# A transformer layer on one core: parameter rows and lambdas behind the first norm's root, and the conditioning's sums over partitions by transposes

## Chip, core and metric

One core of a Trainium2 chip. The metric is the device time of one execution in microseconds; three runs of the kernel before gave 1547.67 us in the median (1547.43 to 1552.2).

## What is computed

One layer over 256 tokens of width 2048 in float32, with adaptive norms: a vector c gives, through a large matrix w_mod, a shift, a scale and a gate for each of the two halves of the layer.

```python
cond = silu(c)
mod = cond @ w_mod[l] + b_mod[l]                       # (1, 6 * 2048)
sh1, sc1, gt1, sh2, sc2, gt2 = split(mod, 6)
u = modulate(rms_norm(h, norm1_g[l]), sh1, sc1)        # norm * (1 + scale) + shift
aq, ak, av, rq, rf, ri, rg, ga, gr = split_columns(u @ w_in[l])
lam = exp(sum(lambda_q1 * lambda_k1)) - exp(sum(lambda_q2 * lambda_k2)) + lam_init
ya = diff_attention(aq, ak, av, lam, subln_g[l], lam_init)
yr = hgrn2(rq, rf, ri, rg, lower_bounds[l], gnorm_g[l])
merged = sigmoid(ga) * (ya @ w_att_out[l]) + sigmoid(gr) * (yr @ w_rec_out[l])
h = h + gt1 * (merged @ w_o[l])
u = modulate(rms_norm(h, norm2_g[l]), sh2, sc2)
h = h + gt2 * ((silu(u @ w_ffn_gate[l]) * (u @ w_ffn_up[l])) @ w_ffn_down[l])
return rms_norm(h, final_g)
```

## The kernel before

Every large product is done three times in float32r: a weight tile w is split into a high part wh (a cast on ScalarE, L240) and a low part wl (a subtraction on VectorE, L242), the left side into uH and uL, and `products` (L245) issues for each k tile of 128 and each of the two token tiles the matmuls uH x wh, uH x wl and uL x wh. Split tiles lie in four buffers each, weights in three, accumulators in four banks (two groups of 512 columns).

**The first norm and its conditioning.** `rstd1` (L348) sums the squares of x on ScalarE, eight activations with accumulation of 128x512, and takes the root in a chain of small VectorE instructions (`rstd_of`, L196). `norm1` (L358) scales x by the root (xn), transposes it on TensorE and copies it to xT. The shift and scale come from `mod_cols` (L391), a generator. It streams its part of w_mod, multiplies each row of 128 by its entry of cond and adds up over k on VectorE into two tiles modc, one for the shift and one for the scale (L403, L407). Each modc holds 128 partial sums per column, one per partition, and these are summed over the partitions by `col_sum` (L333): for each block of 128 columns an fp32 matmul with modc as the weights and a column of ones, which leaves the sums as a column in the bank pmc. Then L426 to L428 add bias, 1 and the norm's gain, and `modulated` (L378) makes u, uH and uL from xT.

**Chunks.** The first seven projections are done in four chunks over k (`kchunks`: 3, 4, 5 and 4 tiles of 128), so that the first can start when a part of the conditioning is there. In a chunk, `chunk_cols` (L467) runs 14 groups of 512 columns with 18, 24, 30 or 24 matmuls each, and while it does, the conditioning of the next chunk runs beside it. That is an order written out by hand: `group` calls `step` (L266) behind the products of each piece of weights; `step` adds `pace["cond"]` to an account and resumes the generator once for each whole unit in it (`advance`, L258). The pace is AHEAD (1.15) times the number of loads over the number of steps (L475). A resumption of `mod_cols` goes as far as the next yield: one load, or one load and the sums for two. Behind the last chunk step `drain` resumes what is left. The conditioning of the second norm (`mod_cols(0, KA, 3, ...)`, L721, and the two of KREST, L842) runs in the same way beside later products, the rows of the gates in `mod_rows`.

The first norm's conditioning of chunk 0 is resumed by hand: two resumptions, then x is loaded, the parameter rows, and the root is taken; then 14 more, of which all but two put their VectorE instructions behind the root's last (`issue_after(last_rstd[0])`, L703). `load_rows` (L139) brings 57 rows of parameters and 96 of b_mod, transposes both on TensorE and copies them to cols and bcols on ScalarE. `lambdas` (L177) loads four vectors and takes two sums and an Exp, then `small_params` (L162) takes a softmax of two rows with another Exp; that generator is appended to the side work.

A planner orders the instructions of each engine: it takes them by the order in which the program traces them, as far as their inputs and buffers are there by its own reckoning, so that one may be moved ahead of another that is still waiting. `issue_after(ins)` puts what the block traces on the engine of `ins` behind it. Each engine works through its queue in order.

Of the kernel before, what the change touches and what calls it, by code (L numbers as in the profile page):

```python
# [8 lines left out]
F32 = mybir.dt.float32  # L9
# [3 lines left out]
AF = mybir.ActivationFunctionType  # L13
# [5 lines left out]
P = 128  # L19
D = 2048  # L20
S = 256
KT = D // P
# [29 lines left out]
def block_kernel(  # L52
# [7 lines left out]
    nc = tc.nc  # L60
# [13 lines left out]
    def bigt(name, dt=F32, n=1):  # L74
        r = [big.tile([P, 1024], dt, tag="big", name=f"{name}{i}") for i in range(n)]
        return r[0] if n == 1 else r

    def bank(name):
        return ps.tile([P, 512], F32, tag="ps", name=name)
# [42 lines left out]
    def quarter(tiles, g):  # L122

        return tiles[g // 2][:, (g % 2) * NG:(g % 2 + 1) * NG]
# [14 lines left out]
    def load_rows():  # L139
        rows = tmp.tile([P, P], F32, tag="side", name="rows", bufs=NS)  # L140
        brows = tmp.tile([P, P], F32, tag="side", name="brows", bufs=NS)
        nc.scalar.dma_start(out=brows[:nbrow, :], in_=b_mod.rearrange("o (k p) -> (o k) p", p=P))
        for r0, n, ap in (
            (0, 16, norm1_g.rearrange("o (k p) -> (o k) p", p=P)),
            (16, 16, norm2_g.rearrange("o (k p) -> (o k) p", p=P)),
            (32, 16, lb_logits.rearrange("o (k p) -> (o k) p", p=P)),
            (48, 8, gnorm_g.rearrange("o h p -> (o h) p")),
            (56, 1, subln_g),
        ):
            nc.scalar.dma_start(out=rows[r0:r0 + n, :], in_=ap)  # L150
        pc = bank("pc")
        nc.tensor.transpose(out=pc[:, :nrow], in_=rows[:nrow, :], identity=ident[:nrow, :nrow])
        nc.tensor.transpose(out=pc[:, P:P + nbrow], in_=brows[:nbrow, :], identity=ident[:nbrow, :nbrow])
        nc.scalar.copy(out=cols, in_=pc[:, :nrow])
        nc.scalar.copy(out=bcols, in_=pc[:, P:P + nbrow])
# [21 lines left out]
    def lambdas():  # L177

        lv = tmpt("lv", S).rearrange("p (i d) -> p i d", d=64)
        for i, ap in enumerate((lambda_q1, lambda_q2, lambda_k1, lambda_k2)):  # L180
            nc.scalar.dma_start(out=lv[:, i, :], in_=ap.to_broadcast([P, 64]))
        for _ in range(6):
            yield
        nc.vector.tensor_mul(out=lv[:, 0:2], in0=lv[:, 0:2], in1=lv[:, 2:4])
        ls = small.tile([P, 2], F32, tag="s2", name="ls")
        nc.vector.reduce_sum(out=ls, in_=lv[:, 0:2], axis=AX.X)
        nc.scalar.activation(ls, ls, AF.Exp)

        nc.vector.tensor_sub(out=lam[:, 0:1], in0=ls[:, 0:1], in1=ls[:, 1:2])
        nc.vector.tensor_scalar_add(out=lam[:, 0:1], in0=lam[:, 0:1], scalar1=LAM_INIT)  # L190
        nc.vector.tensor_scalar_mul(out=lam[:, 1:2], in0=lam[:, 0:1], scalar1=-1.0)
        small_params()
# [3 lines left out]
    def rstd_of(ssq, n, width, name, eps=None):  # L196

        def new(x):
            return small.tile([P, n], F32, tag=f"r{n}", name=name + x, bufs=6)

        v, y = new("v"), new("y")
        if eps is None:
            nc.vector.tensor_scalar(out=v, in0=ssq, scalar1=1.0 / width, scalar2=EPS, op0=ALU.mult, op1=ALU.add)
        else:
            nc.vector.scalar_tensor_tensor(out=v, in0=ssq, scalar=1.0 / width, in1=eps, op0=ALU.mult, op1=ALU.add)
        yi = y.bitcast(I32)
        nc.vector.tensor_single_scalar(out=yi, in_=v.bitcast(I32), scalar=1, op=ALU.arith_shift_right)
        nc.vector.tensor_scalar(out=yi, in0=yi, scalar1=-1.0, scalar2=float(0x5F3759DF), op0=ALU.mult, op1=ALU.add)
        vh = new("h")
        nc.vector.tensor_scalar_mul(out=vh, in0=v, scalar1=-0.5)  # L210
        for i in range(3):
            q, y2 = new(f"q{i}"), new(f"y{i}")
            if n == 1:
                nc.vector.scalar_tensor_tensor(out=q, in0=y, scalar=y, in1=vh, op0=ALU.mult, op1=ALU.mult)
            else:
                nc.vector.tensor_mul(out=q, in0=y, in1=y)
                nc.vector.tensor_mul(out=q, in0=q, in1=vh)
            last_rstd[:] = [nc.vector.scalar_tensor_tensor(out=y2, in0=q, scalar=1.5, in1=y, op0=ALU.add, op1=ALU.mult).ins]
            y = y2
        return y  # L220
# [37 lines left out]
    def advance(queue):  # L258
        while queue:
            try:  # L260
                next(queue[0])
                return
            except StopIteration:
                queue.pop(0)
# [68 lines left out]
    def col_sum(p, j0, a, n):  # L333
        for j in range(n):
            mm(p[:, j0 + j:j0 + j + 1], a[:, j * P:(j + 1) * P], ones[:, 0:1], start=True, stop=True)  # L335
# [6 lines left out]
    def square_sum(dst, src):  # L342
        return nc.scalar.activation(junk[:, :src.shape[-1]], src, AF.Square, accum_out=dst)  # L343

    xT, uH_t, uL_t = [], [], []
    xTv, uH, uL = halves(xT), halves(uH_t), halves(uL_t)

    def rstd1(xt):  # L348

        s8 = small.tile([P, 2, 4], F32, tag="s8", name="ssq")  # L350
        for t in range(2):
            for g in range(4):
                square_sum(s8[:, t, g:g + 1], quarter(xt[t], g))
        s2 = small.tile([P, 2], F32, tag="s2", name="ssq1")
        nc.vector.reduce_sum(out=s2, in_=s8, axis=AX.X)
        return rstd_of(s2, 2, D, "n1")

    def norm1(xt, rr, g):  # L358

        for t in range(2):  # L360
            xn = tmpt("xn")
            nc.scalar.activation(xn, quarter(xt[t], g), AF.Copy, scale=rr[:, t:t + 1])
            p = bank("pxT")
            for j in range(4):
                nc.tensor.transpose(out=p[:, j * P:(j + 1) * P], in_=xn[:, j * P:(j + 1) * P], identity=ident)
            nc.scalar.copy(out=xT[g].rearrange("p (k s) -> p k s", s=S)[:, :, t * P:(t + 1) * P], in_=p.rearrange("p (k s) -> p k s", s=P))
# [24 lines left out]
    def mod_cols(k0, nk, chunk, gcol, src, H, L, after=None, room=0, lag=0):  # L391

        wid = nk * P
        a = [tmp.tile([P, 1024], F32, tag="modc", name=f"modc{ci}", bufs=2) for ci in range(2)]
        waiting = []

        def sums(q, kk, ci, w):
            for j in range(kk):  # L400
                s1, d = cond[:, q + j:q + j + 1], a[ci][:, :wid]
                if q + j == 0:
                    first = nc.vector.tensor_scalar_mul(out=d, in0=w[:, j], scalar1=s1)  # L403
                    if after is not None:
                        tc.add_manual_dep(first.ins, after.ins.name, NOSYNC, reason="the norm goes first")
                else:
                    nc.vector.scalar_tensor_tensor(out=d, in0=w[:, j], scalar=s1, in1=d, op0=ALU.mult, op1=ALU.add)  # L407

        for q, kk in mod_loads(nk):
            for ci in range(2):  # L410
                waiting.append((q, kk, ci, load_mod(q, kk, (chunk + ci) * D + k0 * P, wid, q >= room)))
                if ci == 0:
                    yield
            while len(waiting) > (lag if q < room else 0):
                sums(*waiting.pop(0))
            yield
        for w in waiting:
            sums(*w)
        p = bank("pmc")
        for ci in range(2):  # L420
            col_sum(p, ci * nk, a[ci], nk)
        for _ in range(GAP if chunk else GAP1):
            yield
        ks = slice(k0, k0 + nk)
        bc = [bcols[:, (chunk + ci) * KT + k0:(chunk + ci) * KT + k0 + nk] for ci in range(2)]
        nc.vector.tensor_add(out=sh_col[:, ks], in0=p[:, 0:nk], in1=bc[0])  # L426
        nc.vector.tensor_add(out=sc_col[:, ks], in0=p[:, nk:2 * nk], in1=bc[1])
        nc.vector.scalar_tensor_tensor(out=sc_col[:, ks], in0=sc_col[:, ks], scalar=1.0, in1=gcol[:, ks], op0=ALU.add, op1=ALU.mult)  # L428
        if src is not None:
            for k in range(k0, k0 + nk):  # L430
                modulated(src(k, slice(0, S)), k, H, L)
# [264 lines left out]
    for _ in range(XAT):  # L696
        next(first)
    x1 = load_x()
    load_rows()
    with tc.issue_after(cond_act.ins):  # L700
        r1 = rstd1(x1)
    for i in range(XAT2):
        with tc.issue_after(last_rstd[0]) if i >= 2 else ExitStack():  # L703
            next(first, None)
    side.append(lambdas())
    advance(side)
    xT += bigt("xT", n=4)
    for g in range(4):
        norm1(x1, r1, g)
    uH_t += bigt("uH", F32R, 4)  # L710
    uL_t += bigt("uL", F32R, 4)
    for _ in first:
# [220 lines left out]
```

## Time and profile before

| | |
|---|---|
| median of three runs | 1547.67 us |
| the profiled execution | 1543.71 us, of which its span is 1541.5 us |
| mean granted TensorE clock | 0.998 |
| matmuls (PE) busy | 1495.4 us, 97% |
| weight loads (PEld) busy | 1233.7 us, 80% |
| VectorE (DVE) busy | 1101.4 us, 71% |
| ScalarE (ACT) busy | 732.4 us, 48% |
| DMA | 373.67 MB, 242 GB/s over the span |

The profile is of one execution, 4 us shorter than the median of the runs; what is summed up from its rows is compared with its own time. Busy shares are means over all stages. What an engine waited for, and who waited for it, stands in the views of waits, and the chain of waits follows the end of the program back from each step to what released it.

### The profile page before, as it was taken

Reading aid. Unit: us, or ns where it says so; the run is one execution under the profiler, and the core shown is the slowest. Engines: PE = TensorE matmul, PEld = TensorE weight load, DVE = VectorE, ACT = ScalarE, POOL = GpSimd, SP = SyncE. Lnnn points to the kernel's source line nnn. Section 1 sums busy time; section 2 is a strip of 40 time slices with the busy share of each in tenths; the row PEclk is TensorE's granted clock in tenths of the full one; section 3 lists DMA queues with packets and bytes.
Section 4 is the critical chain, followed back from the end, with each engine's and each line's share of the span. In section 5 each row is a group of like instructions: output and inputs, shape, how many; then the busy total and the mean of one; then the engine's idle time right before and its main releaser. Section 6 shows DMA issues by size and latency. Waiting matters only on the chain.

```text
span 1541.5 us, 18297 instructions
## 1 busy us (share of the span) xinstructions
PE 1495.4 (97%) x6931; PEld 1233.7 (80%) x6931; DVE 1101.4 (71%) x1439; ACT 732.4 (48%) x1015; POOL 10.5 (1%) x40
## 2 busy tenths in 40 slices
PE   3999999999999999999989999999999999999997
PEld 2788888888878778888878888888888888888885
DVE  5789997788877688987578778879555555544555
ACT  5563433524567764444464554444333444444443
POOL 1000000000000000000000000000000000000000
PEclk9999999999999999999999999999999999999999
DMA  9899998444764389899549988868555655556552
GB/s 312 306 327 320 314 322 273 165 137 150 253 239 150 110 306 337 319 333 333 194 156 352 329 316 286 296 222 304 199 196 196 196 180 191 187 187 219 190 194 103
DMA packets 175987, 373.67 MB, mean 242 GB/s; under 512 B 8430, under 2 KB 12695, under 8 KB 175899
## 3 DMA queue, kind: packets, MB, share of 16 engines
q1 hardware_dynamic: 174776, 371.77, 69.9%
q8 instruction: 54, 0.88, 0.2%
q10 hardware_dynamic: 1122, 0.74, 0.2%
q14 instruction: 35, 0.28, 0.0%
HBM read 370.38 MB, written 2.10 MB: 242 GB/s over the span
## 4 chain that ended last, share of the span: by engine, by line
PE 89%; DVE 5%; DMA 3%; ACT 2%; issue 1%; SPq 0%; DVEq 0%; ACTq 0%
PE acc L250 27%; PE acc L251 27%; PE acc L252 27%; PE ptr L504 2%; DMA wm<-in_w_mod_dram 2%; DVE wl L242 2%; PE pl L589 2%; DVE modc L407 1%; PE pmc L335 1%; DMA w<-in_w_in_dram 1%; ACT junk L343 1%; PE psc L652 0%; PE prow L330 0%; PE pav L683 0%; DMA rows<-in_gnorm_g_dram 0%
## 5 line engine op out<-in xcount | busy, mean ns | idle before, releaser
L240 ACT CAST wh<-w 128x1024 fp32r<-128x1024 f32 (+1 forms) x518 | 529.7, 1030 | 673.9 <-PE acc L252 575.5
L242 DVE TENSOR_TENSOR wl<-w,wh 128x1024 fp32r<-128x1024 f32 (+1 forms) x518 | 613.9, 1193 | 324.3 <-ACT wh L240 323.1
L250 PE MATMUL acc<-wh,uH 128*128 128x512 f32 x704 | 277.7, 394 | 2.4 <-ACT uH L383 2.4
L251 PE MATMUL acc<-wl,uH 128*128 128x512 f32 x704 | 276.7, 393 | 0.4 <-DVE wl L242 0.4
L251 PE MATMUL acc<-wl,u2H 128*128 128x512 f32 x704 | 274.4, 390 | 2.8 <-DVE wl L242 2.8
L250 PE MATMUL acc<-wh,u2H 128*128 128x512 f32 x704 | 275.4, 391 | 1.6 <-ACT u2H L794 1.6
L252 PE MATMUL acc<-wh,uL 128*128 128x512 f32 x704 | 276.4, 393 | 0.0
L252 PE MATMUL acc<-wh,u2L 128*128 128x512 f32 x704 | 275.0, 391 | 0.0
L407 DVE SCALAR_TENSOR_TENSOR modc<-wm,cond,modc 128x512 f32<-128x512 f32 (+3 forms) x210 | 166.8, 822 | 18.7 <-DMA wm<-in_w_mod_dram 17.9
L251 PEld LDWEIGHTS acc<-wl,u2H 128*128 128x128 f32 x704 | 132.2, 188 | 30.9 <-DVE wl L242 3.6
L250 PEld LDWEIGHTS acc<-wh,uH 128*128 128x128 f32 x704 | 133.0, 189 | 29.0 <-ACT uH L383 2.5
L251 PEld LDWEIGHTS acc<-wl,uH 128*128 128x128 f32 x704 | 132.8, 189 | 29.0 <-issue 1.2
L252 PEld LDWEIGHTS acc<-wh,uL 128*128 128x128 f32 x704 | 132.8, 189 | 28.2 <-issue 0.6
L250 PEld LDWEIGHTS acc<-wh,u2H 128*128 128x128 f32 x704 | 132.2, 188 | 28.9 <-ACT u2H L794 1.9
L252 PEld LDWEIGHTS acc<-wh,u2L 128*128 128x128 f32 x704 | 132.2, 188 | 27.4 <-DVE u2L L795 0.2
L251 PE MATMUL acc<-wl,fH 128*128 128x512 f32 x352 | 137.4, 390 | 0.0
L252 PE MATMUL acc<-wh,fL 128*128 128x512 f32 x352 | 137.1, 390 | 0.0
L250 PE MATMUL acc<-wh,fH 128*128 128x512 f32 x352 | 137.0, 389 | 0.0
L320 DVE SCALAR_TENSOR_TENSOR gt<-wm,cond,gt 128x1024 f32<-128x1024 f32 x64 | 81.7, 1277 | 7.4 <-DMA wm<-in_w_mod_dram 7.0
L251 PEld LDWEIGHTS acc<-wl,fH 128*128 128x128 f32 x352 | 66.1, 188 | 13.9 <-issue 0.2
L252 PEld LDWEIGHTS acc<-wh,fL 128*128 128x128 f32 x352 | 66.1, 188 | 13.8 <-issue 0.2
L250 PEld LDWEIGHTS acc<-wh,fH 128*128 128x128 f32 x352 | 66.1, 188 | 13.7
(250 smaller groups left out, 1217.6 us busy)
## 6 DMA issues: line engine op xcount, KB each, us to landing
wm<-in_w_mod_dram SPq DMA_DIRECT2D x160, 512.0 KB, 6.0
w<-in_w_in_dram SPq DMA_DIRECT2D x74, 1024.0 KB, 5.5
w<-in_w_ffn_gate_dram SPq DMA_DIRECT2D x44, 1024.0 KB, 5.2
w<-in_w_ffn_up_dram SPq DMA_DIRECT2D x44, 1024.0 KB, 7.9
w<-in_w_ffn_down_dram SPq DMA_DIRECT2D x44, 1024.0 KB, 5.1
w<-in_w_o_dram SPq DMA_DIRECT2D x16, 1024.0 KB, 6.6
w<-in_w_in_dram SPq DMA_DIRECT2D x14, 768.0 KB, 6.4
wm<-in_w_mod_dram SPq DMA_DIRECT2D x32, 320.0 KB, 5.0
```

Source lines behind the costliest of these rows:

```text
L240: nc.scalar.copy(out=wh, in_=src)
L242: nc.vector.tensor_sub(out=wl, in0=src, in1=wh.bitcast(F32))
L250: mm(po[t], aH(k, ts), h, start=first, stop=False)
L251: mm(po[t], aH(k, ts), lo, start=False, stop=False)
L252: mm(po[t], aL(k, ts), h, start=False, stop=last)
L320: nc.vector.scalar_tensor_tensor(out=a[i], in0=w[:, 0], scalar=cond[:, k:k + 1], in1=a[i], op0=ALU.mult, op1=ALU.add)
L335: mm(p[:, j0 + j:j0 + j + 1], a[:, j * P:(j + 1) * P], ones[:, 0:1], start=True, stop=True)
L343: return nc.scalar.activation(junk[:, :src.shape[-1]], src, AF.Square, accum_out=dst)
L407: nc.vector.scalar_tensor_tensor(out=d, in0=w[:, j], scalar=s1, in1=d, op0=ALU.mult, op1=ALU.add)
L504: nc.tensor.transpose(out=p[:, j * P:(j + 1) * P], in_=src[:, j * P:(j + 1) * P], identity=ident)
L589: mm(p[:, (4 * b + j) * 64:(4 * b + j + 1) * 64], kb[:, j, b * P:(b + 1) * P], qb[:, j, b, :, 1, :], start=True, stop=True)
```

## The change

The parameter rows become a generator that yields between its loads and the rest, and so do the lambdas, whose six yields become one. Both are started (their loads issued) before the first norm's squares, and finished behind the fourth xn on ScalarE and behind the root on VectorE. `mod_cols` takes its sums over partitions, in every call but the one for chunk 0 (`room < KT`), in another way: it transposes the blocks of 128 columns, four to a bank, with a yield between banks, and each transposed block is copied on ScalarE with an accumulator, which gives the sums as columns of an SBUF tile.

```diff
@@ load_rows
             nc.scalar.dma_start(out=rows[r0:r0 + n, :], in_=ap)
+        yield
         pc = bank("pc")
@@ lambdas
-        for _ in range(6):
-            yield
+        yield
@@ rstd1, norm1
+    last_square = []
-                square_sum(s8[:, t, g:g + 1], quarter(xt[t], g))
+                last_square[:] = [square_sum(s8[:, t, g:g + 1], quarter(xt[t], g)).ins]
+    xns1 = []
-            nc.scalar.activation(xn, quarter(xt[t], g), AF.Copy, scale=rr[:, t:t + 1])
+            xns1.append(nc.scalar.activation(xn, quarter(xt[t], g), AF.Copy, scale=rr[:, t:t + 1]).ins)
@@ mod_cols
-        p = bank("pmc")
-        for ci in range(2):
-            col_sum(p, ci * nk, a[ci], nk)
+        if room < KT:
+            p = small.tile([P, 2 * nk], F32, tag="mcs", name="mcs", bufs=2)
+            for j0 in range(0, 2 * nk, 4):
+                n = min(4, 2 * nk - j0)
+                pt = bank("pmt")
+                for j in range(n):
+                    ci, k = divmod(j0 + j, nk)
+                    nc.tensor.transpose(out=pt[:, j * P:(j + 1) * P], in_=a[ci][:, k * P:(k + 1) * P], identity=ident)
+                for j in range(n):
+                    nc.scalar.activation(junk[:, :P], pt[:, j * P:(j + 1) * P], AF.Copy, accum_out=p[:, j0 + j:j0 + j + 1])
+                if j0 + n < 2 * nk:
+                    yield
+        else:
+            p = bank("pmc")
+            for ci in range(2):
+                col_sum(p, ci * nk, a[ci], nk)
@@ the first norm
-    load_rows()
+    vectors = [load_rows(), lambdas()]
+    for v in vectors:
+        next(v)
     with tc.issue_after(cond_act.ins):
         r1 = rstd1(x1)
...
-    side.append(lambdas())
-    advance(side)
     xT += bigt("xT", n=4)
     for g in range(4):
         norm1(x1, r1, g)
+    with tc.issue_after(last_rstd[0]), tc.issue_after(xns1[3]):
+        for v in vectors:
+            next(v, None)
```

## Rows read from the trace of the kernel before

**Rows 1.** The page: GB/s in 40 equal slices of the span, and one costly group.

```profile
GB/s 312 306 327 320 314 322 273 165 137 150 253 239 150 110 306 337 319 333 333 194 156 352 329 316 286 296 222 304 199 196 196 196 180 191 187 187 219 190 194 103
...
L240 ACT CAST wh<-w 128x1024 fp32r<-128x1024 f32 (+1 forms) x518 | 529.7, 1030 | 673.9 <-PE acc L252 575.5
```

**Rows 2.** Waits of PE from 40 to 290 us: total us, times, longest.

```profile
PE acc L251 <- DVE wl L242: 0.4, 1, 0.4
```

**Rows 3.** Timeline of PE: start, length in us, instructions [idle before <- released by].

```profile
39.60 0.79 PE L250 MATMUL acc<-wh,uH 128*128 128x512 f32 x1 [2.41 <-ACT uH L383]
...
788.10 0.50 PE L250 MATMUL acc<-wh,u2H 128*128 128x512 f32 x1 [1.62 <-ACT u2H L794]
```

**Rows 4.** Timeline of ACT (ACTq issues loads), the first 40 us.

```profile
1.78 0.98 ACTq L181 DMA_DIRECT2D lv<-in_lambda_q_dram  x2
...
10.87 0.63 ACT L343 ACTIVATE junk<-x 128x512 f32<-128x512 f32 x1 [5.60 <-DMA rows<-in_norm_g_dram]
...
11.63 0.63 ACT L343 ACTIVATE junk<-x 128x512 f32<-128x512 f32 x1
...
15.15 0.64 ACT L343 ACTIVATE junk<-x 128x512 f32<-128x512 f32 x1
...
15.90 1.28 ACT L169 ACT_TABLE_LOAD   x1
...
17.31 0.61 ACT L343 ACTIVATE junk<-x 128x512 f32<-128x512 f32 x1
...
38.16 1.09 ACT L373 ACTIVATE u<-xT,sh_col,sc_col 128x256 f32<-128x256 f32 x2 [2.21 <-DVE sc_col L428]
```

**Rows 5.** Timeline of DVE, 19 to 40 us.

```profile
19.56 0.16 DVE L355 TENSOR_REDUCE ssq<-ssq 128x2 f32<-128x8 f32 x1 [1.31 <-ACT junk L343]
...
22.10 12.79 DVE L407 SCALAR_TENSOR_TENSOR modc<-wm,cond,modc 128x384 f32<-128x384 f32 x24
...
37.23 0.16 DVE L426 TENSOR_TENSOR sh_col<-pmc,bcols 128x3 f32<-128x3 f32 x1 [1.21 <-PE pmc L335]
...
37.97 0.15 DVE L428 SCALAR_TENSOR_TENSOR sc_col<-sc_col,cols 128x3 f32<-128x3 f32 x1
```

**Rows 6.** Timeline of SP's queue: 14 loads of the conditioning.

```profile
7.86 13.56 SPq L225 DMA_DIRECT2D wm<-in_w_mod_dram  x14
```

**Rows 7.** Loads issued up to 40 us: count, KB each, median us to landing.

```profile
wm<-in_w_mod_dram SPq DMA_DIRECT2D x16, 384.0 KB, 7.1
...
x<-in_x_dram SPq DMA_DIRECT2D x4, 512.0 KB, 5.5
```

**Rows 8.** Chain of waits, pieces in order of time: start us, us, what.

```profile
40.39 0.43 PE acc L251
...
45.12 0.23 PE acc L251
...
95.23 1.69 PE pmc L335 x16
...
172.66 2.12 PE pmc L335 x20
...
293.76 1.75 PE ptr L504 x16
...
749.33 3.46 PE pmc L335 x32
...
854.37 1.68 PE pmc L335 x16
```

**Rows 9.** Timeline of ACT: two squares with accumulation on 128 columns.

```profile
468.76 0.28 ACT L343 ACTIVATE junk<-po 128x128 f32<-128x128 f32 x1
...
469.16 0.28 ACT L343 ACTIVATE junk<-po 128x128 f32<-128x128 f32 x1
```

**Rows 10.** Timeline of PE at the sums for chunk 1.

```profile
95.07 1.84 PE L335 MATMUL pmc<-ones,modc 128*128 128x1 f32 x16
96.78 0.49 PE L250 MATMUL acc<-wh,uH 128*128 128x512 f32 x1
```

## Prediction, made before the changed kernel ran

> **What bounds the kernel now.** I read the busy shares of the page first: TensorE's matmul row is busy nearly all of the span and the other engines are not, but that says only that PE's queue is the one to look at. The waits of PE tell more: from 40 us to 290 us, the whole first projection, the only wait behind its first matmul is one of 0.4 us [rows 2]. So there a microsecond taken out of PE's queue is a microsecond of time, and so is one put in. Before 40 us PE has next to nothing to do, and the time at which its first projection matmul starts (39.60 us, after 2.41 us idle) counts in full [rows 3]. Two places matter then: the chain up to 39.60 us, and what stands in PE's queue between the projection's matmuls.
>
> The chain up to 39.60 us, read backwards through the timelines: the first uH comes from u (ScalarE, 38.16 us), u from sc_col (L428, 37.97 us), that from the column sums of chunk 0, and those from 24 modc instructions that run on VectorE without a break from 22.10 us for 12.79 us [rows 4, 5]. They are held behind the root of the first norm by issue_after, and the root's reduction begins at 19.56 us, when the last of eight squares is read. Between the fourth and the fifth square ScalarE copies cols and bcols, which wait for the rows' loads; between the fifth and the sixth it loads a table and does an Exp [rows 4].
>
> **The squares.** Two squares start 0.76 us apart (10.87, 11.63), so the fifth could start at 13.9 but starts at 15.15, and the sixth could start at 15.90 but starts at 17.31 [rows 4]. That is 1.25 + 1.41 = 2.7 us, and the change takes both out: copies, table load and Exp are put behind the fourth xn, their VectorE part behind the root. Three lambda instructions also leave the gaps of the root's chain; they filled latency, which I count as 0.1. The root comes 2.8 us earlier, at 19.4. Two things must not come late instead. x: its four loads take 5.5 us to land and are all issued when the conditioning's 14 loads start at 7.86 [rows 6, 7], so x is there by 13.4, while the seventh square would start at 15.4. The conditioning's weights: 14 loads are issued from 7.86 to 21.42 and land 7.1 us later [rows 6, 7], the last at about 28.5; VectorE would want it for the last two of 24, at 19.4 + 22 x 0.53 = 31.1. Neither binds. The lambdas' four loads already go out ahead of the rows' loads on ScalarE's queue, at 1.78 us [rows 4], so moving them up in the program moves nothing; SP's queue and POOL's aren't passed by anything.
>
> What comes back: on ScalarE at most the same 2.7 us, now between the xn and the first u. It is idle 2.21 us ahead of u [rows 4], so I cost it at nothing up to half a microsecond that would not fit; without that cover it is 2.7 us. On VectorE 13 short instructions at some 0.16 us [rows 5], 2.1 to 2.4 us. If they stand behind the modc run they lie in the wait for the column sums (from 34.9, when the run ends, to L426 at 37.23) and cost little; if the planner puts them into the run they cost all of it. Bounds 0 and 2.4, and as they are traced after the run, I take 0.5. Front: **-2.3 us**, bounds -2.8 and 0. PE is still at half clock when it starts (one matmul each 0.43 us, later 0.23 [rows 8]); that moves along.
>
> **The sums.** Chunk 0 keeps its matmuls. The 58 other sums stand in the chain of waits with 1.69 (8 sums), 2.12 (10), 3.46 (16) and three times 1.68 (8 each, one row stands): 12.31 us, 0.21 us each, as an fp32 matmul is two passes. A transpose of a 128x128 block is one pass: 16 take 1.75 us, 0.109 each [rows 8], so 58 take 6.3 us. PE saves **6.0 us**, all in places where it doesn't wait. The price on ScalarE is a copy with accumulation for each: two such on 128 columns start 0.40 us apart [rows 9], 23 us in all. ScalarE's casts spend 575.5 us of their 673.9 us idle waiting until PE frees a buffer [rows 1], that is, ahead of need, so I cost this work itself at nothing; a cast behind four of them comes 1.6 us later, and where a stretch has less lead than that it costs the difference.
>
> **The resumptions.** This is what I think decides. The generator now yields between groups of four transposes, and the pace isn't raised for that. Chunk 0 resumes chunk 1's conditioning 1.15 x 16 / 14 = 1.314 times per step, 14 steps. Before, the 17th resumption does sums and u, and falls in step 13 (17.1). After, the 17th does the first four transposes only, and the 18th falls in step 14 (18.4), the chunk's last. Chunk 1, with 0.4 carried over and 2.629 per step: 33 wanted before, 34.6 reached in step 13; 35 wanted after, step 14. Chunk 2, with 0.2 and 0.657: 17 before, step 26 of 28; 18 after, step 28. A step comes behind the products of its group. So at all three chunk boundaries the last transposes move from ahead of the last group's 18, 24 and 30 matmuls to behind them, where the next matmul in PE's queue needs their result.
>
> Before, that group is the cover: the sums at 95.07 us are followed by a matmul at 96.78 [rows 10] and PE doesn't wait [rows 2]. After, PE waits for: four transposes 0.44, about 0.2 until the last is out (an estimate: the sums are busy 0.13 us beyond the next matmul's start [rows 10]), four accumulating copies 1.6, L427 and L428 between 0.4 and 0.9 (in the chain of chunk 0 L426 starts at 37.23 and L428 is done at 38.12, with other work between them [rows 5]), and from there 1.48 to the first matmul (38.12 to 39.60 [rows 3, 5]): 4.3 us, of which 0.44 is counted above. Wait **3.9 us**. Chunk 1's last group has only two sums: 0.22 + 0.2 + 0.8 + 0.65 + 1.48, less 0.22, is **3.1**. Together 3.9 + 3.1 + 3.9 = **10.9 us**. Below, the bound is 0 for each, where the planner lifts the transposes ahead of waiting matmuls, as it may. Above, one cast in the way on ScalarE, 1.03 us [rows 1], and about as much on VectorE (an estimate from it) make it 6 each. What is queued behind: on PE the next chunk's matmuls, on ScalarE casts whose buffers are full anyway. Nothing behind gives the wait back, since PE is the engine that sets the pace.
>
> The second norm's conditioning also ends later, but its first part ends near 750 us, some 35 us before PE waits for u2H at 788 [rows 3, 8], and its last has 24 matmuls (5.4 us) of the four k ahead of it as cover (0.23 each [rows 8]), against the 4.3. I cost it at nothing; at worst 1 us.
>
> Sum: -2.3 - 6.0 + 10.9 = **+2.6 us** on the profiled execution's 1543.7 (span 1541.5), so 1546.3. The median of the runs shown lies 4.0 us above that execution; I carry the difference over: 1547.7 + 2.6, **1550.3 us**, 0.17% slower, within the 0.3% (4.6 us) that a measurement of this kernel can tell from none.
>
> **Rivals.** First, *the cover holds*: the planner puts transposes ahead of matmuls that it sees waiting for a weight's split, and PE never waits at a boundary. Then -8.3, 1539.4; with two of three boundaries covered, -1.3. For it: work is moved ahead elsewhere (the lambdas' loads stand before the rows' loads, which are traced earlier [rows 4]). Against it: in the kernel before, the sums of chunk 1 stand behind the group that they are traced behind: from 39.60 to 95.07 us there is just room for 13 groups of 18 matmuls, 11 or 12 of them cold [rows 3, 8, 10].
>
> Second, *the clock falls*, on the slow side. PE's longest pause inside the run is 1.62 us, and the matmul behind it takes 0.50 us, the first one of all 0.79 at half clock [rows 3], 1.2 GHz instead of 2.4. A pause of 4 us occurs nowhere after 40 us, so no row says what follows it. If it drops the clock as at the start, some 11 matmuls run 0.2 us longer [rows 8], 2.2 us per boundary, 6.6 for three: +9.2, 1556.9. It decides from the first boundary at which the pause is long enough. The Trainium skill, "TensorE: Matmul & The Clock Gate", section "Why this matters for your kernels", speaks against this change by the same rule: idle gaps between bursts of matmuls bring half the clock back. The trace shows the half level at the start, and no fall after the gaps that it has. A cast or subtraction in the way at each boundary gives the same side, +3 to +6 more.
>
> Third, *the front is lost*: the VectorE instructions stand in the run, or the feed gives it back. In its six slices up to 231 us DMA moves 306 to 327 GB/s, later up to 352 [rows 1], so the feed has a little room and I don't expect it. +2.3 more, 1552.6. Or the change doesn't do what it says, if something else holds the fifth square: the same time.
>
> **How the numbers follow.** Three waits of 3 to 4 us, whatever their exact size (-2 to +5): 0.48. Cover at one boundary or more: 0.24, of which 0.17 beyond -4.6 us. Clock or queues: 0.20, nearly all beyond +4.6. Front lost: 0.08, half beyond. With the tail of the first case: faster 0.17, same 0.48, slower 0.35. The range goes from the covered case's upper half, 1541, to the falling clock, 1557; the forecast's own is 1545.5 to 1553.
>
> **What would show it.** Squares without a break from 10.9 to 16.9 us, the run of 24 modc from 19.4, the first projection matmul near 37.3. Three waits of PE for uH of 3 to 4 us where a chunk ends, near 99, 176 and 276 us, each behind accumulating copies; matmuls after them 0.23 apart (0.43 would be the clock). Transposes 0.11 apart where sums were 0.21. It is wrong if PE passes the boundaries without a wait, or if the first matmul doesn't move.

## The result and the profile after

The changed kernel takes 1565.9 us (median of four runs) beside 1548.8 us for the kernel before. The medians lie 17.1 us apart; the ratio, taken over all the runs, is 1.0104 [1.0086, 1.0121], some 16 us slower. 1550.3 us was forecast, and 1557 was the upper end of the range. The profiled execution took 1561.7 us (span 1559.5), 18.0 us more than the profiled execution of before.

From the kernel after, the span on its page, and the chain of waits where eight of the new transposes stand in it:

```profile
span 1559.5 us, 18305 instructions
```

```profile
770.25 0.87 PE pmt L430 x8
```

Eight transposes in 0.87 us are 0.109 each, half of what one sum took [rows 8]. PE's queue became shorter as computed. The loss must be in waits; the waits of PE in the kernel after (total us, times, longest us):

```profile
PE acc L250 <- ACT uH L387: 19.7, 4, 6.5
...
PE acc L250 <- DVE part L476: 3.4, 3, 1.8
```

`part` is a projection's sum over the chunks done so far; ScalarE copies it out of the accumulator's bank (L474) and VectorE adds the later chunks to it (L476).

Before, PE waited for uH once, 2.41 us at the start [rows 3], and for anything at all 0.4 us after that up to 290 us [rows 2]. The timeline of PE in the kernel after shows where the four waits are (start, length, instruction, idle before and what released it):

```profile
37.61 0.80 PE L250 MATMUL acc<-wh,uH 128*128 128x512 f32 x1 [3.08 <-ACT uH L387]
...
97.09 0.60 PE L430 MATMUL pmt<-ident,modc 128*128 128x128 f32 x4
104.18 0.80 PE L250 MATMUL acc<-wh,uH 128*128 128x512 f32 x1 [6.50 <-ACT uH L387]
104.78 0.63 PE L251 MATMUL acc<-wl,uH 128*128 128x512 f32 x1
...
188.05 0.38 PE L430 MATMUL pmt<-ident,modc 128*128 128x128 f32 x2
194.56 0.80 PE L250 MATMUL acc<-wh,uH 128*128 128x512 f32 x1 [6.12 <-ACT uH L387]
...
292.87 0.60 PE L430 MATMUL pmt<-ident,modc 128*128 128x128 f32 x4
297.44 0.79 PE L250 MATMUL acc<-wh,uH 128*128 128x512 f32 x1 [3.98 <-ACT uH L387]
```

The reader is to see two things. At each of the three chunk boundaries the last transposes stand directly ahead of a matmul that waits for their result, 6.50, 6.12 and 3.98 us, 16.6 in all. And the matmul behind each wait lasts 0.80 us, the next 0.63, as long as the very first one of the span. The windows of the kernel after give the clock (window, its length, busy time and instructions of PE, PEld, DVE, ACT, POOL, granted clock, DMA share, GB/s):

```profile
104.00:108.00 4.00, 3.82 (x9) 2.91 (x10) 3.65 (x7) 3.09 (x8) 0.00 (x0) 0.50 0.99 356
...
194.00:198.00 4.00, 3.44 (x8) 2.40 (x9) 3.33 (x6) 2.35 (x7) 0.00 (x0) 0.50 0.95 339
...
297.00:300.00 3.00, 2.56 (x6) 2.08 (x7) 1.46 (x4) 2.38 (x7) 0.00 (x0) 0.53 0.90 327
```

0.50 is 1.2 GHz instead of 2.4. Read matmul by matmul, PE works at half clock for 5.2, 3.5 and 3.1 us behind the three waits; half of those 11.8 us, 5.9, are lost.

Both kernels issue the same matmuls for their products, so each can be compared with its counterpart. Against the profiled execution of before, the kernel after is 2.5 us ahead at 45 us, 21.8 us behind at 300 us and 17.8 us behind at the end: all of the loss arises at the chunks, and the rest of the span gives 4 us back.

The front went as forecast. The timeline of VectorE in the kernel after, with the root's reduction, the run of 24 modc and the first of the instructions moved behind it, and that of ScalarE with the last square, the table load and the first u:

```profile
16.99 0.16 DVE L357 TENSOR_REDUCE ssq<-ssq 128x2 f32<-128x8 f32 x1 [1.31 <-ACT junk L343]
...
19.44 12.79 DVE L411 SCALAR_TENSOR_TENSOR modc<-wm,cond,modc 128x384 f32<-128x384 f32 x24
32.14 0.28 DVE L184 TENSOR_TENSOR lv<-lv 128x128 f32<-128x128 f32 x1
```

```profile
16.24 0.63 ACT L343 ACTIVATE junk<-x 128x512 f32<-128x512 f32 x1
...
34.07 1.28 ACT L187 ACT_TABLE_LOAD   x1
...
36.17 1.09 ACT L377 ACTIVATE u<-xT,sh_col,sc_col 128x256 f32<-128x256 f32 x2 [0.50 <-DVE sc_col L445]
```

The run of modc begins 2.66 us earlier than in [rows 5], and the first matmul 1.99 us earlier (37.61 against 39.60 [rows 3]).

### The profile page after: what moved, and what is told of

Same layout as the page of the kernel before. It is cut to its first block, busy times and chain, and to the rows that moved or that the text cites. A ratio compares the mean times of both kernels' runs of the same rounds, so it can differ in the third digit from the quotient of the medians.

```text
span 1559.5 us, 18305 instructions
## 1 busy us (share of the span) xinstructions
PE 1494.7 (96%) x6873; PEld 1229.6 (79%) x6873; DVE 1102.4 (71%) x1439; ACT 753.2 (48%) x1131; POOL 10.9 (1%) x40
## 4 chain that ended last, share of the span: by engine, by line
PE 80%; DVE 8%; DMA 8%; ACT 2%; issue 2%; ACTq 0%; SPq 0%; DVEq 0%
PE acc L250 25%; PE acc L252 25%; PE acc L251 25%; DMA wm<-in_w_mod_dram 5%; DVE wl L242 3%; DVE modc L411 2%; DMA w<-in_w_in_dram 2%; PE ptr L521 2%; PE pl L606 2%; DVE part L476 1%; ACT wh L240 1%; PE psc L669 0%; PE prow L330 0%; ACT junk L343 0%; DMA lv<-in_lambda_q_dram 0%
## 5 line engine op out<-in xcount | busy, mean ns | idle before, releaser
L252 PEld LDWEIGHTS acc<-wh,fL 128*128 128x128 f32 x352 | 66.1, 188 | 13.7 <-issue 0.2
L250 PEld LDWEIGHTS acc<-wh,fH 128*128 128x128 f32 x352 | 66.1, 188 | 13.7
```

Source lines behind the costliest of these rows:

```text
L250: mm(po[t], aH(k, ts), h, start=first, stop=False)
L252: mm(po[t], aL(k, ts), h, start=False, stop=last)
```

## The experiments

Each short diff is against the kernel named. Ratios are to the kernel before, measured on the same chip with the run of the variant.

**The front alone** (the kernel after, with the old sums everywhere).

```diff
-        if room < KT:
...
-        else:
-            p = bank("pmc")
-            for ci in range(2):
-                col_sum(p, ci * nk, a[ci], nk)
+        p = bank("pmc")
+        for ci in range(2):
+            col_sum(p, ci * nk, a[ci], nk)
```

> Only the first part: rows and lambdas behind the root, all sums by matmuls at their old place. Theory (the time is lost at the chunk boundaries, where the last transposes come behind the chunk's last group and PE waits): the first projection matmul at about 37.6 us as in the changed kernel (39.6 before), no wait of PE for uH behind it, and 2 to 3 us less than before, ratio 0.997 to 0.999. Rival (the moved rows and lambdas disturb ScalarE and VectorE in chunk 0): slower than before, ratio over 1.002.

Measured: 1548.88 us beside 1548.88, 0.9999 [0.9989, 1.0010]. In its trace PE waits for uH only at the start (3.5 us), and the work of the second to fourth chunk starts 1.5 to 1.7 us earlier than in the profile of before. By 716 us it is 3.5 us behind. So the front's gain is there in the trace and can't be found in the time. A part of where it went is in the windows of this kernel behind the 16 sums of the second norm:

```profile
756.00:760.00 4.00, 4.00 (x13) 3.17 (x13) 1.54 (x4) 0.00 (x0) 0.00 (x0) 0.57 0.21 39
```

The clock was halved there for 3.4 us with PE busy all the time. The rest (between 412 and 470 and between 580 and 686 us) has no single cause that I could name. It needn't come from the front: the second profile of the unchanged kernel, further down, loses 2.7 us between 412 and 716 us against the first, where this kernel loses 5.

**The sums alone** (the kernel before, with the transposes, copies and yields of the change, without its front).

```diff
-        p = bank("pmc")
-        for ci in range(2):
-            col_sum(p, ci * nk, a[ci], nk)
+        if room < KT:
+            p = small.tile([P, 2 * nk], F32, tag="mcs", name="mcs", bufs=2)
...
+        else:
+            p = bank("pmc")
+            for ci in range(2):
+                col_sum(p, ci * nk, a[ci], nk)
```

> Only the second part: transposes and accumulating copies with their yields, rows and lambdas as before. Theory: the three waits of PE for uH (16.6 us together in the changed kernel) and the half clock behind them are all here; some 19 to 21 us more than before, ratio 1.012 to 1.014. Rival (both parts are needed for the loss): well below the changed kernel's +16, ratio under 1.006.

Measured: 1566.8 us, 1.0127 [1.0102, 1.0152]. PE's waits for uH at the boundaries are 7.34, 6.09 and 3.98 us, nearly those of the whole change. The whole loss comes with the sums; the front isn't needed for it.

**The change without its yield** (the kernel after; the transposes of a chunk come in one resumption).

```diff
-                if j0 + n < 2 * nk:
-                    yield
```

> The changed kernel without the yield between groups of transposes, so that all of them, and u, fall in the same resumption as the sums before. Theory: the resumption is what decides; no wait of PE for uH at a boundary over 1 us, no half clock after 45 us, and the time comes to the front (-2.5) and the shorter sums (-6.0): 1540 us, ratio 0.993 to 0.996. Rival (the 58 accumulating copies, 23 us of ScalarE, hold up the casts): PE waits for casts and splits, and it stays above before, ratio over 1.003.

Measured: 1544.8 us, 0.9987 [0.9972, 1.0001]. Without the yield the whole loss is gone, and 2 us more (1.0104 - 0.9987 = 0.0117, some 18 us). It didn't reach the 0.993 to 0.996 expected. Its waits of PE tell why (total us, times, longest us):

```profile
PE acc L250 <- ACT uH L387: 6.0, 2, 3.1
PE acc L250 <- ACT part L472: 2.8, 1, 2.8
```

and from its timeline of PE, the wait for `part` at the first boundary:

```profile
99.91 0.50 PE L250 MATMUL acc<-wh,uH 128*128 128x512 f32 x1 [2.77 <-ACT part L472]
```

The matmul behind that wait lasts 0.50 us, and the clock stays at full speed. Of the 6.0 us for uH, 3.0 are the start's; 2.96 are at the second boundary (180.87 us), where the ten copies ran only from 173.59 us, behind casts, and there the clock was low for 6.8 us. So ScalarE's copies aren't free even where the transposes are early.

**The late place alone** (the kernel before, its matmul sums kept, and as many empty yields put ahead of them as the change adds).

```diff
+        if chunk == 0 and room < KT:
+            for _ in range((2 * nk - 1) // 4):
+                yield
         p = bank("pmc")
```

> The kernel before with as many empty resumptions ahead of the matmul sums of chunks 1 to 3 as the change adds (1, 2, 1): no transpose, no accumulating copy, only the later place. Theory: PE waits for uH at all three boundaries, each for L426 to L428 and the way to uH, 2.5 to 4 us, and 7 to 12 us are added, up to 7 more if the pause drops the clock: ratio 1.005 to 1.012. Rival (transposes and copies are the cause): within 2 us of before, ratio 0.999 to 1.001.

Measured: 1562.4 us, 1.0095 [1.0075, 1.0114]. No transpose, no copy, and a net loss nearly as large. In its timeline of PE the sums for the second chunk stand where the transposes stood, and the next matmul waits, as it does at the two other boundaries:

```profile
98.94 1.84 PE L335 MATMUL pmc<-ones,modc 128*128 128x1 f32 x16
103.05 0.79 PE L250 MATMUL acc<-wh,uH 128*128 128x512 f32 x1 [2.28 <-ACT uH L383]
...
187.47 0.79 PE L250 MATMUL acc<-wh,uH 128*128 128x512 f32 x1 [2.43 <-ACT uH L383]
...
288.80 0.50 PE L250 MATMUL acc<-wh,uH 128*128 128x512 f32 x1 [2.41 <-ACT uH L383]
```

The three waits are 2.28, 2.43 and 2.41 us, 7.1 in all, and the clock is halved at all three, for 6.8, 3.4 and 3.4 us; PE works for 5.9, 3.3 and 3.4 us of that. 7.1 + 12.6 / 2 = 13.4 us, beside 13.5 between the medians. The net losses are alike, but not what they are made of. This kernel keeps the old front and the old sums, while the change loses some 26 us at the boundaries and in the waits for `part` (16.6 + 5.9 + 3.4) and earns the rest back. So the place by itself accounts for about half of what the change loses there. The other half is longer waits, with transposes and copies on the way.

**The pause filled** (the kernel after, with four fp32 matmuls whose result nobody reads behind the last transposes of each chunk).

```diff
+                elif chunk == 0:
+                    fill = bank("fill")
+                    for _ in range(4):
+                        mm(fill, ones, xT[0][:, :NG], start=True, stop=True)
```

> The changed kernel with four fp32 matmuls of ones on xT (128x512, result unused) behind the last transposes of chunks 1 to 3, some 3.4 us of PE work in a pause of 6.5, 6.1 and 4.0 us. Theory (the pauses let the clock fall, and that is a part of the loss of its own): PE waits for uH 3 us each less, the start of the next chunk stays where it is, no half clock at 102, 191 and 297 us, and 4 to 7 us less than the changed kernel: ratio 1.006 to 1.008 against before. Rival (the half clock costs nothing, as the feed would hold PE up anyway): within 1.5 us of the changed kernel, ratio 1.0095 to 1.0115.

Measured: 1555.8 us, 1.0037 [1.0022, 1.0052]. The windows of this kernel behind the fill at the first and the second boundary:

```profile
104.00:107.00 3.00, 2.90 (x7) 2.32 (x8) 2.90 (x5) 2.48 (x8) 0.00 (x0) 0.51 0.97 356
...
188.00:192.00 4.00, 3.29 (x14) 2.74 (x15) 2.99 (x7) 3.01 (x6) 0.00 (x0) 1.00 0.93 300
```

The fill lasts 3.60 us each time. At two boundaries the clock now stays, at the first it falls for 3.4 us; there the fill ends at 101.5 us and the matmul that PE waits for starts at 104.10, 2.63 us later (0.34 and 0.54 at the others). The ratio drops by 0.0067, some 10 us, more than the 4 to 7 expected. The clock gives back some 4.4 of its 5.9 us. The waits for `part` (3.4 us) are gone as well, and pause and fill together last 6.2, 3.9 and 4.1 us where the waits were 6.50, 6.12 and 3.98, so that uH comes 2.2 us earlier at the second boundary. The run therefore doesn't measure the clock by itself, and why the two other terms go with the fill wasn't tested.

**The pace counts the yields** (the kernel after).

```diff
-            pace["cond"] = AHEAD * 2 * len(mod_loads(kchunks[ci + 1][1])) / nsteps
+            pace["cond"] = AHEAD * (2 * len(mod_loads(kchunks[ci + 1][1])) + (2 * kchunks[ci + 1][1] - 1) // 4) / nsteps
```

> The changed kernel with a pace that counts the added resumptions, so that sums and u come in steps 13, 13 and 25 again. Theory (place decides first, and what the kernel without yields still lost, some 3 us at each of the first two boundaries, is ScalarE's queue: copies of part and u behind eight to ten accumulating copies): no wait at the third boundary, up to 3 us at the first two, 1543 to 1547 us, ratio 0.996 to 0.999. Rival (the yields themselves cost, wherever they fall): over 1.004.

Measured: 1541.65 us beside 1550.3, 0.9945 [0.9932, 0.9958]. 0.996 to 0.999 was expected. From its timeline of PE, the first and the second boundary:

```profile
93.97 1.03 PE L430 MATMUL pmt<-ident,modc 128*128 128x128 f32 x8
94.76 0.48 PE L250 MATMUL acc<-wh,uH 128*128 128x512 f32 x1
...
101.89 0.79 PE L250 MATMUL acc<-wh,uH 128*128 128x512 f32 x1 [2.77 <-ACT part L474]
...
175.21 0.38 PE L430 MATMUL pmt<-ident,modc 128*128 128x128 f32 x2
175.34 0.48 PE L250 MATMUL acc<-wh,uH 128*128 128x512 f32 x1
```

The transposes have a group's matmuls behind them again, and no wait for uH is left but that of the start. One wait for `part` (2.77 us, as without the yield) and one fall of the clock (101.9 us, 3.4 us long) remain. With the same yields, transposes and copies as the change this is 8.6 us faster than the kernel before: without the late place there is no loss.

**Transposes in the second norm only** (the kernel after).

```diff
-        if room < KT:
+        if chunk == 3:
```

> The changed kernel with transposes only in the second norm's conditioning (32 sums) and matmuls in chunks 0 to 3: front as changed, boundaries as before. Theory: no wait behind 40 us that before doesn't have; sums 3.5 us shorter, front 1.5 to 2.5: 4 to 6 us less than before, ratio 0.996 to 0.998, and faster than the kernel without yields. Rival (the front's gain doesn't reach the end, since the front alone measured 0.9999): 3 us at most, ratio 0.998 to 0.9995.

Measured: 1541.8 us, 0.9950 [0.9935, 0.9965], better than the 0.996 to 0.998 expected. Sums of chunks 1 to 3 are matmuls where they were; 32 of the 58 are transposes. Against the front alone that is some 8 us for 32 x 0.1 = 3.2 us of PE time. The trace shows no fall of the clock from 43 to 1534 us, which led to the next two runs.

**The kernel before once more**, unchanged, for a second profile.

> The kernel before once more, with a profile: how far two executions of one kernel differ between 400 and 1100 us, where the front alone lost 7 us against the first profile. If that loss is the spread of executions, this one is up to 6 us behind the first profile in that stretch too; if it comes from the front's change, it stays within 1 us of it.

Measured: 1553.3 us, span 1551.1, against 1543.7 and 1541.5 of the execution that the prediction read. Its timeline of PE at the second norm's 16 sums:

```profile
754.99 4.68 PE L335 MATMUL pmc<-ones,modc 128*128 128x1 f32 x32
759.54 0.77 PE L250 MATMUL acc<-wh,mH 128*128 128x512 f32 x1
```

The same 32 instructions took 3.46 us in the first profile [rows 8] and were followed by matmuls at full clock. Here the clock halves within them, with no pause of PE, and stays down for 6.8 us. It also fell for 3.4 us at 177.1, behind the ten sums for the third chunk. Half of 10.2 us, some 5 of the 9.6 us between the two executions of one kernel, are these; of the rest, 2.7 us lie between 412 and 716 us and are open.

**The second norm's sums issued twice** (the kernel before).

```diff
         for ci in range(2):
-            col_sum(p, ci * nk, a[ci], nk)
+            for _ in range(2 if chunk else 1):
+                col_sum(p, ci * nk, a[ci], nk)
```

> The kernel before with the one-column sums of the second norm (32 of 64) issued twice, same result. PE work is 6.8 us more. Theory (a run of one-column matmuls, though PE is busy, lets the clock fall, as one of the two profiles of before shows at 757 us): the 16 sums issued twice take 7 us and more, the profile shows half clock behind them, and 8 to 13 us are added, ratio 1.005 to 1.0085. Rival (PE that is busy keeps its clock, and the fall at 757 us has another cause): no half clock there, 6.8 us added, ratio 1.0035 to 1.005.

Measured: 1563.2 us, 1.0084 [1.0064, 1.0103], 13 us for 32 more sums that are 6.7 us by 0.21 each. Its chain of waits has

```profile
752.42 10.91 PE pmc L335 x64
```

where twice 3.46 would be 6.9, and its windows there

```profile
757.00:761.00 4.00, 4.00 (x20) 4.00 (x21) 0.00 (x0) 0.00 (x0) 0.00 (x0) 0.50 0.00 0
761.00:765.00 4.00, 4.00 (x15) 3.66 (x16) 1.54 (x4) 0.00 (x0) 0.00 (x0) 0.50 0.00 0
```

PE is busy all through, and the clock is halved, 13.7 us long here and 3.4 behind each of the two shorter groups of sums. So a run of one-column fp32 matmuls can bring the clock down although PE doesn't pause. It doesn't each time (in the first profile of before it didn't), but where it does, such a sum costs more than its own time.

**Transposes from the third chunk on, with a pace that counts them** (the kernel after).

```diff
-        if room < KT:
+        if room == 0:
...
-            pace["cond"] = AHEAD * 2 * len(mod_loads(kchunks[ci + 1][1])) / nsteps
+            pace["cond"] = AHEAD * (2 * len(mod_loads(kchunks[ci + 1][1])) + (2 * kchunks[ci + 1][1] - 1) // 4 * (ci > 0)) / nsteps
```

> The changed kernel with transposes in chunks 2 and 3 and the second norm, matmul sums for chunks 0 and 1, and the pace of chunks 1 and 2 counting the added resumptions. Theory: the wait for part at the first boundary (2.8 us in the kernel with the pace over all) and its half clock go, the third boundary keeps that kernel's gain: 1 to 3 us less than either of the two faster kernels, ratio 0.992 to 0.995 against before. Rival (accumulating copies at the second boundary cost as much as the sums that they replace): ratio 0.995 to 0.997.

Measured: 1543.1 us, 0.9954 [0.9937, 0.9971]. Meant to join the best of the two variants above (0.992 to 0.995), it equals them; all three lie within each other's intervals. The wait for `part` at the first boundary and the half clock behind it are gone from its trace, as expected, and the time isn't shorter.

## Why the prediction was wrong, step by step

| step | forecast, us | profile after, us |
|---|---|---|
| front: first matmul earlier | -2.3 | -2.0, and 0.7 less of half clock at the start |
| 58 sums | -6.0 | -6.0 (0.109 each) |
| three waits at chunk boundaries | 3.9 + 3.1 + 3.9 = 10.9 | 6.50 + 6.12 + 3.98 = 16.6 |
| half clock behind them | 0, +6.6 as a rival | 5.9 |
| waits for `part` in the second chunk | not forecast | 3.4 |
| sum | +2.6 | +17.2 of the measured 18.0 |

The steps that failed are the size of the three waits (10.9 us forecast, 16.6 in the trace), the half clock, which was held as a rival at nothing in the sum (5.9 us, on top of the waits), and the accumulating copies at nothing (3.4 us of waits for `part`, whose cause is open).

**Front.** Right in every row forecast: squares without a break to 16.9, the run of modc from 19.4, the small instructions behind it, the first matmul at 37.6 for 37.3. That it is worth 2 us at the end is not shown: alone, it measured 0.9999.

**Resumptions.** Right that they decide, and right about all three places: the counting of steps held, and the transposes stand behind the last group. The empty yields, the missing yield and the counted yields show it from three sides (1.0095, 0.9987, 0.9945). Of the rival in which the cover holds, one sum is misread: -1.3 us is one boundary of three covered (-8.3 + 7.0); two covered would give -4.4 to -5.2.

**The size of the waits: the first mis-sized term.** The forecast laid the copies end to end behind the transposes. It put nothing ahead of them and nothing between, and spoke of casts only as queued behind. The third boundary came to 3.98 us for 3.9, partly by luck: a cast stands ahead of the first copy there too, and the steps on VectorE were shorter than assumed. The timeline of ScalarE in the kernel after, at the three boundaries:

```profile
97.53 1.04 ACT L240 CAST wh<-w 128x1024 fp32r<-128x1024 f32 x1 [1.86 <-DMA w<-in_w_in_dram]
98.48 0.27 ACT L432 ACTIVATE junk<-pmt 128x128 f32<-128x128 f32 x1
...
98.75 1.03 ACT L240 CAST wh<-w 128x1024 fp32r<-128x1024 f32 x1
99.68 0.28 ACT L432 ACTIVATE junk<-pmt 128x128 f32<-128x128 f32 x1
...
102.74 1.09 ACT L377 ACTIVATE u<-xT,sh_col,sc_col 128x256 f32<-128x256 f32 x2 [1.90 <-DVE sc_col L445]
...
187.82 1.13 ACT L240 CAST wh<-w 128x512 fp32r<-128x512 f32 x2
188.85 0.28 ACT L432 ACTIVATE junk<-pmt 128x128 f32<-128x128 f32 x1
...
293.06 1.05 ACT L240 CAST wh<-w 128x1024 fp32r<-128x1024 f32 x1 [1.67 <-PE acc L252]
294.02 0.27 ACT L432 ACTIVATE junk<-pmt 128x128 f32<-128x128 f32 x1
```

At the first boundary the last transpose ends at 97.7 us. A cast for the next weights, which had waited for its load, holds the first copy until 98.48, and a second cast stands between the copies: some 1.4 us together. At the second boundary casts hold the last two copies by some 0.4 us. Then VectorE, at the first two:

```profile
100.55 1.22 DVE L242 TENSOR_TENSOR wl<-w,wh 128x1024 fp32r<-128x1024 f32 x1
101.68 0.16 DVE L444 TENSOR_TENSOR sc_col<-mcs,bcols 128x4 f32<-128x4 f32 x1
101.76 0.88 DVE L411 SCALAR_TENSOR_TENSOR modc<-wm,cond,modc 128x640 f32<-128x640 f32 x1
102.55 0.15 DVE L445 SCALAR_TENSOR_TENSOR sc_col<-sc_col,cols 128x4 f32<-128x4 f32 x1
...
188.60 1.54 DVE L411 SCALAR_TENSOR_TENSOR modc<-wm,cond,modc 128x512 f32<-128x512 f32 x2
190.05 0.68 DVE L242 TENSOR_TENSOR wl<-w,wh 128x512 fp32r<-128x512 f32 x1
190.66 1.28 DVE L476 TENSOR_TENSOR part<-acc,part 128x512 f32<-128x512 f32 x2
191.85 0.68 DVE L242 TENSOR_TENSOR wl<-w,wh 128x512 fp32r<-128x512 f32 x1
192.45 0.16 DVE L444 TENSOR_TENSOR sc_col<-mcs,bcols 128x5 f32<-128x5 f32 x1
```

At the first boundary the two short steps that u waits for stand behind a subtraction of 1.22 us, a modc of 0.88 between them: some 1.2 us more than forecast. At the second the copies are done at 189.6 us, but the next short step starts at 192.45, behind two modc, two subtractions and two additions to `part`: 2.8 us, nearly all of the excess there. So the first wait grew on both engines and the second on VectorE. The prediction knew of this ("one cast in the way on ScalarE, 1.03 us [rows 1], and about as much on VectorE") and gave 6 us for each as the bound. Two of three lay just above that bound, 6.50 and 6.12, far from the value taken. 16.6 - 10.9 = 5.7 us.

**The clock: the second.** The rival named the right mechanism, and its price came close (6.6 for 5.9). That it came so close is one execution's: with the sums alone, behind nearly the same pauses, the clock was low for 10.2, 10.2 and 6.8 us, and PE worked through 17 us of it, 8.5 us lost. "TensorE: Matmul & The Clock Gate" of the Trainium skill, section "Why this matters for your kernels", says that gaps between bursts of matmuls bring back half the clock; the trace now agrees, with 0.50 behind pauses of 6.5 and 6.1 us and 0.53 behind 4.0. What was wrong is how the two were joined: clock and queues were weighed as alternatives to the forecast, and the range ended at the clock alone (1557), without the "+3 to +6 more" of the queues. They are not alternatives. In the kernel after the clock fell in or behind every one of the lengthened pauses, so both came together, and the sum -2.3 - 6.0 + 16.6 + 5.9 = +14.2 lay outside the range. Three pauses of some 4 us after which the clock stays, the case taken as likeliest, had no row for them; the longest that the trace of before had to show was 1.62 us [rows 3].

**The copies, costed at nothing.** Without any late resumption they still left waits of 2.96 us for uH and 2.8 for `part` (the run without the yield). The change's own 3.4 us for `part` may be of this kind: PE waits 2.8 to 3.9 us for `part` in four of the five kernels that have copies in the second chunk's conditioning (the filled pause is the fifth) and at most 0.5 in those that have none. These waits are of two sorts, though. In the kernel after and with the sums alone there are three, for VectorE's `part` within the second chunk; without the yield and with the counted yields there is one, for ScalarE's at the first boundary. Through which engine the copies do it is not settled.

**The sums, -6.0.** Right in PE time and, by what the variants show, too small in time: a run of one-column sums also costs clock, in some executions. The variant with transposes in the second norm only has 32 x 0.1 = 3.2 us less on PE than the front alone and is some 8 us faster. In the trace of the front alone the clock falls for 3.4 us behind these sums, 1.7 us lost, and in the variant's it doesn't; that makes 4.9 us, and the rest is open.

**The time before.** I carried the 4.0 us between the median and the profiled execution over as a constant. It is none: that execution was one in which the clock didn't fall behind the sums, and a second one of the same kernel, in which it did, took 9.6 us more, some 5 of them by the clock. In the seven kernels with transposes in the second norm the clock falls behind them in no trace. So a comparison with this one execution is a hard one: the kernel with the counted yields is 8.6 us faster by the medians, and its profile is 2.8 us shorter than this.

## What to carry to other kernels

A `yield` put into a generator that is resumed at a set pace moves everything behind it: count the resumptions against the pace, and keep one group of matmuls between the last step and its first reader. Where a change takes such cover away, read what stands ahead in the queue of every engine on the path, waiting for loads too, and add the clock on top of the wait rather than beside it. Sums over partitions by one-column matmuls can cost TensorE's clock as well as its time. Transposes with accumulating copies were the better form here once the place was kept: three variants with them are some 0.5% faster, the new front included, which measured nothing by itself.

## What was not expected of the hardware

Sixteen one-column fp32 sums (32 instructions, 3.46 us at full clock) were followed by a granted clock of 0.50 in one execution of the unchanged kernel and in that of the front alone, and not in another of the unchanged kernel; 64 instructions in a row brought it too, and took 10.9 us instead of 6.9. Eight transposes of 128x128 in a row (0.87 us) were followed by full clock in six kernels, and sixteen in a row in the one without the yield.

The length of a pause alone didn't decide. Pauses of 2.3 to 2.4 us behind one-column sums were followed by half clock three times of three. A pause of 2.77 us for `part` at the first boundary was followed by it in the kernel with the counted yields, and not in the one without the yield. The pauses of 1.6 us ahead of u2H and of 1.84 us for `part` were not.
